# Depthwise convolution of a two-layer encoder: from a mix of PE and DVE taps to paired taps on PE alone

## The chip, the core and the metric
One core of one Trainium2 chip. The metric is device time in microseconds (us), from the first to the last instruction of one launch and what lies around it, as the median of several runs. PE is TensorE, PEld its weight loads, DVE VectorE, ACT ScalarE, POOL GpSimd; SP issues nearly all transfers.

## The reference
256 tokens of 1024 channels go through two layers. Each has a token-mixing part and a channel-mixing part (a dense SwiGLU in layer 0, the two best of eight experts in layer 1). The token mixing projects the normalised input to three groups that are computed apart and joined by one output projection: a pooling mixer (256 channels), a Conformer convolution (384 channels), and a spatial gate (384 channels). The convolution is what changes:

```python
def conformer_conv(p, conv_w, conv_b, ln_g, ln_b):     # p: (1, 256, 768), conv_w: (31, 384)
    val, gate = jnp.split(p, 2, axis=-1)
    glu = val * jax.nn.sigmoid(gate)
    y = depthwise_conv(glu, conv_w, width 31, padding 15) + conv_b
    return jax.nn.silu(layer_norm(y, ln_g, ln_b))
```

All is in float32.

## The kernel before, in words
The program is one straight list per engine. A scheduler orders each engine's instructions in advance by their place in the program and by when it thinks their inputs are ready; on the chip every engine runs its list in order and waits on semaphores. Buffers of one name are handed out in program order.

Weights come from memory in chunks of up to 1 MB into a ring of eleven buffers named `raw` (L109). A chunk for a precise product is split by ACT and DVE into a high and a low part (`wh`, L122, and `wl`, L123), and each product is three matmuls (`mm3`, L131 to L133). The modulation of the layers (`ada`) is a matrix-vector product that DVE accumulates chunk by chunk (L184; for the first quarters of layer 0 L256 and L259) and PE sums over partitions (L204, L265).

`mix_layer` (L327) is the token mixing, run once in each layer. In layer 0 its input projection is woven with the first modulation by the list `START` (`m` a quarter of the modulation, `h` a quarter of the hidden state, `A` and `B` chunks of the input projection); in layer 1 the chunks come one after the other, with modulation chunks between by `TICKS1`. With channels on partitions, 384 channels are three tiles `ct` of 128 x 256 tokens. The value half is copied to `glu` by ACT (L417), the sigmoid of the gate half goes to `mf` (L423), and POOL multiplies the two in place (L425), with 15 zero columns on each side.

Then come the spatial gate (L457 to L512), the convolution (L514 to L539), the pooling mixer (L541 to L570, on POOL but for one matmul, L566, and with `pd` in the two-buffer name `mf`), and the layer norm of the convolution: transposes (L576), statistics and normalisation on DVE with a small POOL part (L450 to L454), transposes back (L582), swish (L585) and `put`, which splits into high and low (L474, L475). The output projection takes its k-tiles in the order 6, 7, 0, 1, 4, 5, 2, 3; tiles 2 to 4 are the convolution's.

The convolution has two forms. The first `nchain` tiles (one in layer 0, two in layer 1) are a chain of 31 DVE operations each. For the others ACT scales the identity by one tap's weights, a diagonal of 128 x 128 per tap (L532), in two `raw` buffers per tile, and PE accumulates 31 matmuls over shifted views of `glu` (L536):

```python
dg.append(dt[:, j % 16 * P:(j % 16 + 1) * P])
nc.scalar.activation(out=dg[j], in_=ident, func=AF.Copy, scale=cl[:, w0 + j:w0 + j + 1])
...
nc.tensor.matmul(out=p[:, :S], lhsT=dg[j], rhs=glu[:, ct, j:j + S], start=j == 0, stop=j == TAPS - 1)
```

In the second layer's experts, half of the experts are narrow: two weight matrices are multiplied by the same 64 columns, into the two partition halves of one output (L1039).

Of the kernel before, what the change touches and what calls it, by code (L numbers as in the profile page):

```python
# [40 lines left out]
TICKS0, NCHAIN0 = (0, 0, 0, 0, 0, 0, 0, 0, 2, 2, 2, 2, 0), 1  # L41
TICKS1, NCHAIN1 = (0, 1, 0, 1, 1, 1, 1, 1, 1, 1), 2
# [5 lines left out]
NCOL = 48 + 8 + 8 + 2 + 3 * TAPS + 15  # L48
C_ADAB, C_MIXG, C_FFNG, C_PSC, C_CW = 0, 48, 56, 64, 66
C_CB = C_CW + 3 * TAPS  # L50
# [4 lines left out]
def trunk(ctx: ExitStack, tc: tile.TileContext, t, out):  # L55
# [28 lines left out]
    nc.vector.memset(mhalf, -0.5)  # L84

# [241 lines left out]
    def mix_layer(l, xn, ticks, nchain):  # L327
        cl = cols[l]
        with tc.tile_pool(name=f"mix{l}", bufs=1) as mp:
# [34 lines left out]
            glu = mp.tile([P, CT, S + TAPS - 1], F32, name="glu")  # L364
            nc.gpsimd.memset(glu, 0.0)
            if l:
# [5 lines left out]
                slab(t["in_last"][0], CW, 4, vals)  # L372
            else:
# [27 lines left out]
                for what in START:  # L401
                    q = int(what[1])
                    if what[0] == "m":
                        ada_first(q)
                    elif what[0] == "h":
                        hidden(xn, G, Sh, hh, hl, kps=(q,))
                        if q == 0:
                            heat(bank("dn"), 8)
                    elif what[0] == "A":
                        quarter(q, 0, ((0, vals, False), (CW, gates, False)))  # L410
                    else:
                        quarter(q, 1, ((CW, vs, True), (0, us, False)))
                spare["bank"] = "gu"
                later_ada()
            ds = vals
            for ct in range(CT):
                nc.scalar.copy(out=glu[:, ct, 15:15 + S], in_=ds[ct][0])  # L417
            ds = gates
            if l:
                slab(t["in_last"][1], CW, 4, ds)  # L420
            for ct in range(CT):
                sg = small.tile([P, S], F32, name="mf")
                nc.scalar.activation(out=sg, in_=ds[ct][0], func=AF.Sigmoid)  # L423
                gl = glu[:, ct, 15:15 + S]
                nc.gpsimd.tensor_tensor(out=gl, in0=gl, in1=sg, op=ALU.mult)  # L425
# [89 lines left out]
            for ct in range(nchain):  # L515
                w0 = C_CW + ct * TAPS
                nc.vector.tensor_scalar(out=cv[:, ct], in0=glu[:, ct, 0:S],
                                        scalar1=cl[:, w0:w0 + 1],
                                        scalar2=cl[:, C_CB + ct:C_CB + ct + 1],
                                        op0=ALU.mult, op1=ALU.add)  # L520
                for j in range(1, TAPS):
                    nc.vector.scalar_tensor_tensor(out=cv[:, ct], in0=glu[:, ct, j:j + S],
                                                   scalar=cl[:, w0 + j:w0 + j + 1], in1=cv[:, ct],
                                                   op0=ALU.mult, op1=ALU.add)
            for ct in range(nchain, CT):
                w0 = C_CW + ct * TAPS
                dg = []
                for j in range(TAPS):
                    if j % 16 == 0:
                        dt = raw.tile([P, CH], F32, name="raw")  # L530
                    dg.append(dt[:, j % 16 * P:(j % 16 + 1) * P])
                    nc.scalar.activation(out=dg[j], in_=ident, func=AF.Copy,  # L532
                                         scale=cl[:, w0 + j:w0 + j + 1])
                p = bank()
                for j in range(TAPS):
                    nc.tensor.matmul(out=p[:, :S], lhsT=dg[j], rhs=glu[:, ct, j:j + S],  # L536
                                     start=j == 0, stop=j == TAPS - 1)
# [4 lines left out]
            for ct in range(2):  # L542
# [16 lines left out]
                pd = small.tile([P, S], F32, name="mf")  # L559
# [49 lines left out]
    mix_layer(0, xn, TICKS0, NCHAIN0)  # L609
# [102 lines left out]
    mix_layer(1, xn, TICKS1, NCHAIN1)  # L712
# [531 lines left out]
```

## Time and profile before

| | |
|---|---|
| runs | 1353.39 us median of 3 (1353.2 to 1358.18) |
| the profiled execution | 1357.15 us, its span 1355.1 us |
| busy share of the span | PE 95%, PEld 69%, DVE 64%, ACT 47%, POOL 6% |
| granted TensorE clock | 0.977 in the mean |
| memory traffic | 466.15 MB, 344 GB/s in the mean |

Times in the rows count from the span's start. The first mixing layer ends near 138, the dense SwiGLU near 348, the second mixing layer near 457; the experts take the rest. Matmuls are pipelined, so the records of neighbours overlap: start to start tells the pace. One float32 matmul leaves two records. A granted clock of 1.00 is 2.4 GHz; a mean between 0.5 and 1 is a stretch with both levels.

### The profile page before, as it was taken

How to read it: one execution, taken by the hardware profiler on the slowest of the kernel's cores; microseconds unless marked ns; L12 is line 12 of the kernel's file. 1: busy time of each engine (PE TensorE's matmuls, PEld its weight loads, DVE VectorE, ACT ScalarE, POOL GpSimd, SP SyncE). 2: the span in 40 equal slices, each digit the busy share in tenths (PEclk: the TensorE clock that was granted, in tenths of full speed). 3: DMA queues.
4: the chain of work that ended last, by engine and by line, in shares of the span. 5: the costliest groups of instructions: out<-in, count | busy, mean ns of one | idle time of the engine just before them, and what ended most of it. 6: DMA issues, size and time to landing. Idle time of an engine off the chain costs nothing. (4 is left out here: it accounts for less than half of the span.)

```text
span 1355.1 us, 17989 instructions
## 1 busy us (share of the span) xinstructions
PE 1291.0 (95%) x6684; PEld 936.3 (69%) x6684; DVE 862.3 (64%) x1032; ACT 633.6 (47%) x919; POOL 77.1 (6%) x106
## 2 busy tenths in 40 slices
PE   6998899999897999999999999999999999999995
PEld 6986899998896888853368874447885336886431
DVE  6898886778698699850078873038885008876302
ACT  3563544434481587731257752237773125765101
POOL 1143100000125100000000000000000000000000
PEclk9998999999897999999999999999999999999997
DMA  9855895985573499989999998999998999999894
GB/s 372 318 223 209 341 401 191 401 306 193 206 280 126 176 345 374 354 325 422 421 421 421 393 348 358 421 421 421 421 401 345 410 420 421 421 419 363 367 420 163
DMA packets 71412, 466.15 MB, mean 344 GB/s; under 512 B 8596, under 2 KB 11284, under 8 KB 18968
## 3 DMA queue, kind: packets, MB, share of 16 engines
q1 hardware_dynamic: 71320, 464.95, 85.6%
q8 instruction: 54, 0.88, 0.3%
q14 instruction: 38, 0.31, 0.1%
HBM read 463.87 MB, written 1.05 MB: 343 GB/s over the span
## 5 line engine op out<-in xcount | busy, mean ns | idle before, releaser
L123 DVE TENSOR_TENSOR wl<-raw,wh 128x1024 fp32r<-128x1024 f32 (+1 forms) x454 | 528.1, 1206 | 99.3 <-ACT wh L122 92.8
L122 ACT CAST wh<-raw 128x1024 fp32r<-128x1024 f32 (+1 forms) x454 | 445.0, 1034 | 134.4 <-PE gu L132 45.0
L1039 PE MATMUL gu<-raw,big 128*64 128x512 f32 x896 | 204.9, 595 | 0.0
L1028 PE MATMUL gu<-wl,big 128*128 128x512 f32 x448 | 176.7, 394 | 3.0 <-DVE wl L123 2.5
L1026 PE MATMUL gu<-wh,big 128*128 128x512 f32 x448 | 175.2, 391 | 0.0
L1068 DVE TENSOR_TENSOR maf<-mx,mf 128x256 f32<-128x256 f32 x28 | 11.9, 425 | 231.0 <-PE dn L908 196.7
L1039 PEld LDWEIGHTS gu<-raw,big 128*64 128x64 f32 x896 | 63.1, 137 | 121.6 <-issue 119.8
L1023 PE MATMUL gu<-wh,big 128*128 128x512 f32 x448 | 142.5, 397 | 0.0
L131 PE MATMUL gu<-big,wh 128*128 128x256 f32 x464 | 133.0, 290 | 1.7 <-ACT big L299 1.3
L133 PE MATMUL gu<-big,wl 128*128 128x256 f32 x464 | 132.1, 286 | 0.6 <-DVE wl L123 0.6
L132 PE MATMUL gu<-big,wh 128*128 128x256 f32 x464 | 132.2, 286 | 0.0
L908 PE MATMUL dn<-raw,maf 128*64 128x512 f32 x448 | 110.2, 598 | 0.6 <-DVE maf L1068 0.6
L1042 ACT COPY mg<-gu 128x512 f32<-128x512 f32 x28 | 16.4, 585 | 196.8 <-PE gu L1039 196.8
L1028 PEld LDWEIGHTS gu<-wl,big 128*128 128x128 f32 x448 | 84.3, 188 | 26.1 <-DVE wl L123 7.8
L184 DVE SCALAR_TENSOR_TENSOR acc<-raw,cond,acc 128x1024 f32<-128x1024 f32 x74 | 97.3, 1315 | 1.0
L1023 PEld LDWEIGHTS gu<-wh,big 128*128 128x128 f32 x448 | 82.9, 189 | 19.8 <-ACT wh L122 3.2
L1026 PEld LDWEIGHTS gu<-wh,big 128*128 128x128 f32 x448 | 84.5, 189 | 16.9
L132 PE MATMUL dn<-wl,mah 128*128 128x512 f32 x224 | 91.1, 407 | 1.6 <-DVE wl L123 1.6
L131 PEld LDWEIGHTS gu<-big,wh 128*128 128x128 f32 x464 | 90.4, 196 | 3.1 <-ACT big L299 1.9
L133 PEld LDWEIGHTS gu<-big,wl 128*128 128x128 f32 x464 | 90.3, 195 | 0.8 <-DVE wl L123 0.8
L132 PEld LDWEIGHTS gu<-big,wh 128*128 128x128 f32 x464 | 90.4, 195 | 0.6 <-issue 0.2
L133 PE MATMUL dn<-wh,mal 128*128 128x512 f32 x224 | 88.9, 397 | 0.0
(235 smaller groups left out, 1577.7 us busy)
## 6 DMA issues: line engine op xcount, KB each, us to landing
raw<-in_experts SPq DMA_DIRECT2D x336, 1024.0 KB, 11.7
raw<-in_ada_pairs SPq DMA_DIRECT2D x24, 1024.0 KB, 7.6
raw<-in_ada_w SPq DMA_DIRECT2D x16, 1024.0 KB, 9.2
raw<-in_ffn_w_down SPq DMA_DIRECT2D x11, 1024.0 KB, 7.4
raw<-in_ffn_w_gate SPq DMA_DIRECT2D x10, 1024.0 KB, 11.1
raw<-in_ffn_w_up SPq DMA_DIRECT2D x10, 1024.0 KB, 9.0
raw<-in_w_out SPq DMA_DIRECT2D x8, 1024.0 KB, 6.9
raw<-in_in_first SPq DMA_DIRECT2D x8, 768.0 KB, 17.6
```

The source lines that it names most:

```text
L122: behind(lambda: nc.scalar.copy(out=h, in_=s), on_act)
L123: behind(lambda: nc.vector.tensor_tensor(out=l, in0=s, in1=f32(h), op=ALU.subtract), on_dve)
L131: nc.tensor.matmul(out=o, lhsT=lh, rhs=rh, start=first, stop=False, skip_group_check=True)
L132: nc.tensor.matmul(out=o, lhsT=lh, rhs=rl, start=False, stop=False, skip_group_check=True)
L133: return nc.tensor.matmul(out=o, lhsT=ll, rhs=rh, start=False, stop=last, skip_group_check=True)
L184: nc.vector.scalar_tensor_tensor(out=acc[0], in0=c[:, a], scalar=cond[:, k:k + 1], in1=acc[0], op0=ALU.mult, op1=ALU.add)
L908: nc.tensor.matmul(out=ds[0][q * HALF:(q + 1) * HALF], lhsT=a[:, 2 * i + h], rhs=w[:, h, q * 512:(q + 1) * 512], start=j == 0 and i == 0 a ...
L1023: nc.tensor.matmul(out=p, lhsT=eh[:, k], rhs=wh[a2], start=k == 0, stop=False, skip_group_check=True)
L1026: nc.tensor.matmul(out=p, lhsT=el[:, k], rhs=wh[a2], start=False, stop=False, skip_group_check=True)
L1028: nc.tensor.matmul(out=p, lhsT=eh[:, k], rhs=wl[a2], start=False, stop=k == KT - 1, skip_group_check=True)
L1039: nc.tensor.matmul(out=p[h * HALF:(h + 1) * HALF], lhsT=ef[:, k], rhs=w[:, a], start=k == 0, stop=k == KT - 1, skip_group_check=True)
L1042: nc.scalar.copy(out=g, in_=p)
```

## The change
All three tiles go to PE in both layers. `glu` gets a copy for each half of a tile's 128 channels; in each copy the 64 channels stand twice, on partitions 0 to 63 as they are and on 64 to 127 one token earlier, so that one matmul over 128 partitions applies two taps. A diagonal is then 128 x 64: two 64 x 64 diagonals above each other. 31 taps and a zero tap are 16 pairs, and the two channel halves are matmuls into the two partition halves of one output. The diagonals of one tile (32 x 64 columns) fill one `raw` buffer and are made by one POOL multiplication of a fixed pattern `twice` by the weights, both broadcast. The product of value and sigmoid is made by DVE from PSUM, four operations per tile, instead of ACT's copy and POOL's product. `pd` gets its own two buffers.

```diff
-TICKS0, NCHAIN0 = (0, 0, 0, 0, 0, 0, 0, 0, 2, 2, 2, 2, 0), 1
-TICKS1, NCHAIN1 = (0, 1, 0, 1, 1, 1, 1, 1, 1, 1), 2
+TICKS0 = (0, 0, 0, 0, 0, 0, 0, 0, 2, 2, 2, 2, 0)
+TICKS1 = (0, 1, 0, 1, 1, 1, 1, 1, 1, 1)
+PAIRT = (TAPS + 1) // 2
...
+    twice = const.tile([P, HALF], F32, name="twice")
+    nc.vector.tensor_tensor(out=twice, in0=ident[:, :HALF], in1=ident[:, HALF:], op=ALU.add)
...
-            glu = mp.tile([P, CT, S + TAPS - 1], F32, name="glu")
-            nc.gpsimd.memset(glu, 0.0)
+            glu = mp.tile([P, CT, 2, S + TAPS - 1], F32, name="glu")
+            for edge in (slice(0, 15), slice(14 + S, S + TAPS - 1)):
+                nc.gpsimd.memset(glu[:, :, :, edge], 0.0)
+            dgs = []
+
+            def diagonals():
+                for ct in range(CT):
+                    dg = raw.tile([P, CH], F32, name="raw").rearrange("p (m i) -> p m i", i=HALF)
+                    w0 = C_CW + ct * 2 * PAIRT
+                    nc.gpsimd.tensor_tensor(
+                        out=dg, in0=twice[:, None, :].to_broadcast([P, 2 * PAIRT, HALF]),
+                        in1=cl[:, w0:w0 + 2 * PAIRT].unsqueeze(2).to_broadcast([P, 2 * PAIRT, HALF]),
+                        op=ALU.mult)
+                    dgs.append(dg)
...
                 slab(t["in_last"][0], CW, 4, vals)
+                diagonals()
...
+                    if what == "h3":
+                        diagonals()
...
-            ds = vals
-            for ct in range(CT):
-                nc.scalar.copy(out=glu[:, ct, 15:15 + S], in_=ds[ct][0])
-            ds = gates
             if l:
-                slab(t["in_last"][1], CW, 4, ds)
+                slab(t["in_last"][1], CW, 4, gates)
             for ct in range(CT):
                 sg = small.tile([P, S], F32, name="mf")
-                nc.scalar.activation(out=sg, in_=ds[ct][0], func=AF.Sigmoid)
-                gl = glu[:, ct, 15:15 + S]
-                nc.gpsimd.tensor_tensor(out=gl, in0=gl, in1=sg, op=ALU.mult)
+                nc.scalar.activation(out=sg, in_=gates[ct][0], func=AF.Sigmoid)
+                for h in range(2):
+                    hs = slice(h * HALF, (h + 1) * HALF)
+                    for o in range(2):
+                        nc.vector.tensor_tensor(out=glu[o * HALF:(o + 1) * HALF, ct, h, 15 - o:15 - o + S],
+                                                in0=vals[ct][0][hs], in1=sg[hs], op=ALU.mult)
...
-            for ct in range(nchain):
...
-            for ct in range(nchain, CT):
...
+            for ct in range(CT):
                 p = bank()
-                for j in range(TAPS):
-                    nc.tensor.matmul(out=p[:, :S], lhsT=dg[j], rhs=glu[:, ct, j:j + S],
-                                     start=j == 0, stop=j == TAPS - 1)
+                for m in range(PAIRT):
+                    for h in range(2):
+                        nc.tensor.matmul(out=p[h * HALF:(h + 1) * HALF, :S], lhsT=dgs[ct][:, h * PAIRT + m],
+                                         rhs=glu[:, ct, h, 2 * m:2 * m + S], start=m == 0,
+                                         stop=m == PAIRT - 1, skip_group_check=True)
...
-                pd = small.tile([P, S], F32, name="mf")
+                pd = mp.tile([P, S], F32, name="pd", bufs=2)
```

The table of weights is laid out anew on the host to fit, with the zero tap.

## Rows read from the trace of the kernel before

**Rows 1.** The page: the span, and PE's busy time, its share of the span and its records.

```profile
span 1355.1 us, 17989 instructions
...
PE 1291.0 (95%) x6684; PEld 936.3 (69%) x6684; DVE 862.3 (64%) x1032; ACT 633.6 (47%) x919; POOL 77.1 (6%) x106
```

**Rows 2.** Busy time by stretch: the stretch, its length, then for each engine busy us and records, the granted clock, the DMA share and GB/s.

```profile
101.00:107.00 6.00, 2.54 (x13) 1.80 (x12) 5.96 (x5) 1.35 (x3) 5.08 (x4) 1.00 0.97 400
107.00:110.00 3.00, 3.00 (x12) 2.52 (x11) 2.93 (x3) 2.00 (x4) 1.65 (x2) 0.57 1.01 429
320.00:340.00 20.00, 20.00 (x126) 17.98 (x126) 18.03 (x17) 7.11 (x8) 0.00 (x0) 1.00 0.40 137
422.00:430.00 8.00, 2.75 (x7) 1.76 (x7) 8.00 (x11) 0.86 (x2) 3.33 (x5) 0.68 0.06 8
```

**Rows 3.** Groups of instructions by line and shape, from 0 to 110 us (layer 0): busy us and mean ns of one, then the idle time before them.

```profile
L532 ACT ACTIVATE raw<-ident,cols 128x128 f32<-128x128 f32 x62 | 18.8, 393 | 0.0
L522 DVE SCALAR_TENSOR_TENSOR cv<-glu,cols,cv 128x256 f32<-128x256 f32 x30 | 18.5, 617 | 0.9
...
L506 DVE SCALAR_TENSOR_TENSOR mf<-gu,cols,sgb 64x256 f32<-64x256 f32 x6 | 2.9, 482 | 0.8 <-POOL big L475 0.6
```

**Rows 4.** PE's timeline in layer 0: start, duration, the instructions, and in brackets the idle time before them and what ended it.

```profile
74.31 26.94 PE L536 MATMUL gu<-glu,raw 128*128 128x256 f32 x124
...
106.30 0.70 PE L566 MATMUL gu<-mf,pw 128*128 128x256 f32 x2 [3.46 <-POOL mf L564]
...
113.71 0.52 PE L582 MATMUL gu<-ident,tok 128*128 128x128 f32 x3 [2.40 <-DVE tok L454]
...
118.30 0.39 PE L131 MATMUL dn<-wh,big 128*128 128x512 f32 x1
...
123.53 0.40 PE L133 MATMUL mx<-wh,big 128*128 128x512 f32 x1
...
136.41 1.84 PE L204 MATMUL gu<-ones_c,acc 128*128 128x1 f32 x16
```

**Rows 5.** The same in layer 1; the last row is the last matmul of the output projection.

```profile
407.90 13.55 PE L536 MATMUL gu<-glu,raw 128*128 128x256 f32 x62
...
427.35 0.79 PE L132 MATMUL dn<-wl,big 128*128 128x512 f32 x1 [5.25 <-DVE wl L123]
...
432.81 1.33 PE L576 MATMUL gu<-ident,cv 128*128 128x128 f32 x5 [2.07 <-DVE cv L522]
...
457.18 0.40 PE L133 MATMUL mx<-wh,big 128*128 128x512 f32 x1
```

**Rows 6.** Who waited for whom from 0 to 130 us: us in total, times, the longest.

```profile
POOL acc L191 <- PE dn L265: 29.0, 1, 29.0
...
POOL mf L562 <- PE gu L566: 13.3, 1, 13.3
...
DVE mod L226 <- PE dn L265: 7.3, 4, 1.8
...
PE dn L265 <- DVE acc L259: 0.6, 2, 0.3
```

**Rows 7.** Weight loads of a narrow expert, two to a row.

```profile
660.00 0.14 PEld L1039 LDWEIGHTS gu<-raw,big 128*64 128x64 f32 x2 [0.29 <-issue]
660.43 0.14 PEld L1039 LDWEIGHTS gu<-raw,big 128*64 128x64 f32 x2 [0.29 <-issue]
```

**Rows 8.** POOL and DVE beside each other: POOL's product by its line (ns, min/median/max), then POOL's and DVE's timelines; first L184 and L123 while POOL was idle, then both at 379, then the taps without POOL (397.66) and with it (413.52).

```profile
L425 POOL TENSOR_TENSOR glu<-glu,mf x6: 639/1126/1712, 61.6 to 382.0; 128x256 f32<-128x256 f32 x6
...
55.89 1.82 DVE L123 TENSOR_TENSOR wl<-raw,wh 128x768 fp32r<-128x768 f32 x2
...
162.30 1.28 DVE L184 SCALAR_TENSOR_TENSOR acc<-raw,cond,acc 128x1024 f32<-128x1024 f32 x1
...
379.46 3.89 POOL L425 TENSOR_TENSOR glu<-glu,mf 128x256 f32<-128x256 f32 x3 [26.14 <-ACT mf L423]
...
378.57 2.86 DVE L184 SCALAR_TENSOR_TENSOR acc<-raw,cond,acc 128x1024 f32<-128x1024 f32 x2
381.36 2.80 DVE L123 TENSOR_TENSOR wl<-raw,wh 128x768 fp32r<-128x768 f32 x2
...
397.66 11.56 DVE L522 SCALAR_TENSOR_TENSOR cv<-glu,cols,cv 128x256 f32<-128x256 f32 x29
...
413.52 12.64 DVE L522 SCALAR_TENSOR_TENSOR cv<-glu,cols,cv 128x256 f32<-128x256 f32 x16
```

**Rows 9.** SP's timeline (its DMA issues) where chunks go to the ring, and the ACT cast that first needs one of the three chunks issued from 21.89 on.

```profile
21.89 5.00 SPq L109 DMA_DIRECT2D raw<-in_in_first  x3
...
31.25 0.33 SPq L109 DMA_DIRECT2D raw<-in_in_pool  x1
...
319.69 3.44 SPq L109 DMA_DIRECT2D raw<-in_in_last  x2
324.56 0.38 SPq L109 DMA_DIRECT2D raw<-in_ada_w  x1
...
43.40 0.83 ACT L122 CAST wh<-raw 128x768 fp32r<-128x768 f32 x1
```

**Rows 10.** The end of the dense SwiGLU: the last accumulation on DVE that PE's L204 sums, and that L204.

```profile
336.67 1.28 DVE L184 SCALAR_TENSOR_TENSOR acc<-raw,cond,acc 128x1024 f32<-128x1024 f32 x1
...
340.46 1.84 PE L204 MATMUL gu<-ones_c,acc 128*128 128x1 f32 x16
```

More of the change, by code (lines that the diff above doesn't have):

```diff
@@ L46 @@
 PRE, POST = 3, 1
-NCOL = 48 + 8 + 8 + 2 + 3 * TAPS + 15
+PAIRT = (TAPS + 1) // 2
+NCOL = 48 + 8 + 8 + 2 + 2 * CT * PAIRT + 15
 C_ADAB, C_MIXG, C_FFNG, C_PSC, C_CW = 0, 48, 56, 64, 66
-C_CB = C_CW + 3 * TAPS
+C_CB = C_CW + 2 * CT * PAIRT
 C_LG, C_LB, C_SG, C_SB = C_CB + 3, C_CB + 6, C_CB + 9, C_CB + 12
@@ L325, in quads, with mix_layer @@
         return bank(name).rearrange("p (a s) -> p a s", a=2)
-    def mix_layer(l, xn, ticks, nchain):
+    def mix_layer(l, xn, ticks):
         cl = cols[l]
@@ L514, in mix_layer @@
             cv = mp.tile([P, CT, S], F32, name="cv")
-            for ct in range(nchain):
[L516 to L524, printed above, removed]
-            for ct in range(nchain, CT):
-                w0 = C_CW + ct * TAPS
-                dg = []
-                for j in range(TAPS):
[L529 to L533, printed above, removed]
-                p = bank()
-                for j in range(TAPS):
-                    nc.tensor.matmul(out=p[:, :S], lhsT=dg[j], rhs=glu[:, ct, j:j + S],
-                                     start=j == 0, stop=j == TAPS - 1)
+            for ct in range(CT):
+                p = bank()
+                for m in range(PAIRT):
[3 more added lines that the diff above has]
+                                         stop=m == PAIRT - 1, skip_group_check=True)
                 nc.scalar.activation(out=cv[:, ct], in_=p[:, :S], func=AF.Identity,
@@ L607, in later_ada @@
         ada(0, "2", "3A")
-    mix_layer(0, xn, TICKS0, NCHAIN0)
+    mix_layer(0, xn, TICKS0)
     tick(len(queue), done=True)
@@ L711, in trunk @@
     nc.sync.dma_start(out=rb, in_=t["router_b"].broadcast_to([P, NE]))
-    mix_layer(1, xn, TICKS1, NCHAIN1)
+    mix_layer(1, xn, TICKS1)
     tick(len(queue), done=True)
@@ L1176, in col @@
         return _np.ascontiguousarray(v.reshape(v.shape[0], -1, P).transpose(0, 2, 1))
-    cw = a["conv_w"].transpose(0, 2, 1).reshape(DEPTH, CT, P, TAPS).transpose(0, 2, 1, 3)
+    taps = _np.zeros((DEPTH, 2 * PAIRT, CT * P), a["conv_w"].dtype)
+    taps[:, :TAPS] = a["conv_w"]
+    cw = taps.reshape(DEPTH, PAIRT, 2, CT, 2, HALF).transpose(0, 2, 5, 3, 4, 1)
     cols = _np.concatenate(
         [col(a["ada_b"]), col(a["mix_norm_g"]), col(a["ffn_norm_g"]), col(a["pool_scale"]),
-         cw.reshape(DEPTH, P, CT * TAPS), col(a["conv_b"]), col(a["conv_ln_g"]), col(a["conv_ln_b"]),
+         cw.reshape(DEPTH, P, 2 * CT * PAIRT), col(a["conv_b"]), col(a["conv_ln_g"]), col(a["conv_ln_b"]),
          col(a["sgu_ln_g"]), col(a["sgu_ln_b"])],
```

## The prediction
> **What bounds the kernel now.** I read the page first, then the busy time by stretch around the two convolutions, then PE's timeline there, then the waits, and last the DVE and POOL timelines wherever both were busy. The page says PE 1291.0 us of a span of 1355.1 [rows 1]. So PE is the engine to follow, and a gain has to shorten PE's work or one of its few gaps. Everything behind the second mixing layer (the experts) starts when that layer ends, and its loads pass through the same ring of places, so I carry each shift one to one to the end.
>
> Layer 0: from 74.31 PE runs 124 records of the convolution, 62 matmuls, in 26.94 us without a gap [rows 4], that is 0.434 us a matmul. ACT beside it builds 62 diagonals and DVE does 30 of the 31 taps of the third channel tile [rows 3]. Then PE waits 3.46 us for POOL, and later 2.40 us for the norm on DVE [rows 4]. The first wait starts further back: POOL's L562 waited 13.3 us for PE's L566 [rows 6], because `pd` of the second pooling tile needs the buffer that the first matmul, queued behind the convolution, still reads. After the gap the granted clock is 0.57 in the mean [rows 2], so part of the stretch runs at the lower of the two levels, 1.2 instead of 2.4 GHz.
>
> Layer 1: PE does one tile in 13.55 us, then waits 5.25 and 2.07 us [rows 5] for DVE, which is busy all of 422 to 430 while PE is busy 2.75 of 8 us [rows 2]: two DVE chains of taps set the end here.
>
> **PE's part.** The change needs 3 tiles x 16 tap pairs x 2 halves = 96 matmuls a layer. The narrow experts already run two column halves side by side: two 64-column loads start every 0.43 us with 512 columns streaming [rows 7]; one fp32 matmul is two such records, so a pair costs 0.86 there and 0.43 at 256 columns. Bounds for a pair: 0.43; 0.56 if its four loads of 0.14 came one behind the other and set the pace; 0.86 if the halves did not overlap. I take 0.44, nearest to the row of the same form: 48 x 0.44 = 21.1 us a layer.
> - Layer 0: 26.94 - 21.1 = 5.8 us gained.
> - Layer 1: 21.1 - 13.55 = 7.6 us more.
> The Trainium skill, "TensorE: Matmul & The Clock Gate", Part 3, says that a weight load overlaps a running matmul only when the row group differs; here both halves use all rows. The loads of rows 7 start inside running matmuls of the same rows, so the trace disagrees. What the rule would do is a rival below.
>
> **PE's gaps.** One output-projection matmul costs (123.53 - 118.30) / 23 = 0.227 us at full clock, so the 96 of a layer 21.8. In layer 0 the stretch from 101.25 (end of the convolution) to 136.41 is 35.2 us; with pooling, transposes and the gate's broadcast I count 25.3 of work at full clock, so 9.9 are waste: 3.46 + 2.40 idle and some 4.0 of half clock, split by me as 2.1 and 1.9 behind the two gaps.
> - `pd` gets its own two buffers, so the first gap goes: 3.46 + 2.1 = 5.6 us. The next in line is the norm chain, about 10 us behind the convolution; covered by 5 k-tiles x 12 matmuls x 0.227 = 13.6 us of projection that needs no convolution, if they stand in front of it in PE's order. In the trace they only partly do, hence the 2.40. I take half of that waste: 2.1 us. Bounds 0 and 4.3.
> - Layer 1: from 421.4 to the end of the last projection matmul are some 36.0 us for 24.0 of work (the same without the broadcast) [rows 5]; 12.0 are wasted, 7.3 of them idle, and DVE's chains are the cause. I leave a norm gap of 2.1 and gain 9.9. Less the 7.6 above: 2.3 us.
> Gains so far: 5.8 + 5.6 + 2.1 + 2.3 = 15.8 us.
>
> **What the change takes back: POOL.** Three multiplications of 128x2048 a layer. The nearest row is 128x256 in 0.64 us at best [rows 8], so 8 x 0.64 = 5.1 each and 15.4 us a layer alone. (The Trainium skill, "GPSIMD Engine Reference", section 3.1, gives 4497 ns for a two-input operation of that length: 13.5 a layer, and the sum below would be about 1 us better. No run here shows that shape.)
> But POOL does not run alone. From 379.46 three POOL operations took 3.89 us, double their best, and DVE beside them needed 2.86 and 2.80 us for what costs 2.56 and 1.82 elsewhere [rows 8]: DVE lost 1.28 us, a third of the overlap. Small DVE operations lose more: 16 taps in 12.64 us against 29 in 11.56 [rows 8], about half. At the first price, with POOL overlapping contending DVE work for some 18 us, DVE loses 6 us a layer.
> When? The operations take three places of the raw ring, in program order, as soon as these come free.
> - Layer 0: that is where the loads at 21.89 (three in_first chunks) were issued [rows 9], so POOL works from about 22 to 46. There DVE sums the modulation, PE multiplies it out at once (PE waited only 0.6 for DVE, DVE 7.3 us for PE's four answers [rows 6]) and the next hidden state needs it: a loop without slack, so I charge all 6.
> - Layer 1: places come free at 319.69 to 324.56 [rows 9], so POOL works from 320 to 344, beside DVE at 18.03 of 20 us [rows 2]. The last accumulation, at 336.67, ends 2.6 us before PE's L204 at 340.46 [rows 10] uses it: 6 - 2.6 = 3.4 us.
> Bounds a layer: 0 (POOL gives way, or runs in DVE's gaps) to half of 30.7 us, 15.3.
>
> **The rest.** The displaced loads go to the next free places: the three in_first chunks from 21.89 to about 30 to 36 (before, the ring's next issue is at 31.25); ACT first casts one at 43.40 [rows 9], so I cost it at nothing; without that cover it is a few us. Behind the new POOL work stands the memset of L191, which before sat 29.0 us waiting for PE [rows 6]; SP's transfer into the same tile waits for it, and behind that on SP stand the next modulation chunks and the spatial gate's tables. None of them is used before the convolution's neighbours, so I cost this at nothing; without that cover it is up to some 5 us. Later the ring is better off: three held places instead of four in layer 0. ACT loses 62 and 31 diagonals, on no path now. DVE gets 12 half-tile products of 0.48 [rows 3], 5.8 us a layer, ahead of weight splits in its order, and loses the taps; I charge 1 us in all, bounds 0 and 5. The memset, copies and `twice` are nothing.
>
> **Sum.** 15.8 - 6 - 3.4 - 1 = 5.4 us. The profiled execution took 1357.15 (span 1355.1), 3.8 above the median of the runs, 1353.39; I subtract from the median: 1348.0.
>
> **Rivals.**
> - *POOL gives way* (DVE loses little): for it, that POOL doubled its time at 379.46. 1353.4 - 14.8 = 1338.6. Chance 0.25.
> - *The norm takes the place of the gaps*: PE's order is fixed in advance, and in both layers the second transposes come too early, at their present 2.40 plus half clock. The half that I credited falls away in layer 0 (2.1) and as much again in layer 1 (2.2): gains 5.8 + 5.6 + 0.1, less 10.4: 1352.3. Chance 0.13.
> - *Contention wins*, the slower side: the loss at the price of the taps, half of 30.7 us a layer, 15.3 + 12.7 = 28 against 14.8: up to 1366.6. It decides from a total loss above 14.8 us; for it rows 8's taps, against it that DVE's operations from 22 to 46 are long ones. Chance 0.18.
> - *The halves do not run side by side* as said: 41.3 us a layer, 1348 + 40.4 = 1388. Against it rows 7. Chance 0.03. With the loads unhidden as well, 48 x (0.43 + 0.56) a layer, 1401: chance 0.01. That is the skill's rule on row groups, named above.
> My forecast has the remaining 0.40; its own range is 1343 to 1353.
>
> **How the numbers follow.** About 0.5% (6.8 us, so 1346.6 and 1360.2) is what a measurement of this kernel can tell from no change. Faster: 0.24 of the first rival and 0.18 of the forecast: 0.42. Slower: 0.16 of the contention rival and the 0.04: 0.20. Same: the rest, 0.38. The range reaches from just under the first rival, 1336, to 1360, in the middle of the contention rival.
>
> **What would show it.** Right: conv matmuls 128x64 in 20 to 22 us a layer; no wait of L562 for L566; POOL tensor products of 5 to 10 us at 22 and 320; modulation loop longer than before between 22 and 50; PE's wait at L204 in front of layer 1. Wrong: PE's pace in the conv above 0.5 us a pair; POOL's products at another time, or as quick as 5.1 beside busy DVE; no later end of the input projection.

## The result, and the profile after

The changed kernel took 1365.97 us in the median of its runs (1365.19 to 1368.49), the kernel before 1355.79 beside it (1353.2 to 1358.28): a ratio of 1.0077, with a 95% interval of 1.0056 to 1.0098. That is slower by 10 us, and outside the range of the forecast. The profiled execution took 1366.27, its span is 1364.5. First the page's span and first part, where [rows 1] stand for the kernel before.

```profile
span 1364.5 us, 18241 instructions
...
PE 1292.0 (95%) x6882; PEld 928.3 (68%) x6882; DVE 837.2 (61%) x964; ACT 606.3 (44%) x823; POOL 94.5 (7%) x108
```

PE is busy for as long as before, on more and narrower records. DVE has 25 us less work, ACT 27 less, POOL 17 more. Nothing in these sums is a loss, so the time went into waits. Busy time by stretch (columns as in [rows 2]):

```profile
20.00:40.00 20.00, 13.45 (x76) 13.24 (x76) 15.77 (x17) 4.33 (x7) 11.69 (x3) 0.67 0.84 344
...
320.00:340.00 20.00, 17.74 (x124) 16.29 (x122) 19.58 (x9) 7.92 (x9) 12.84 (x3) 1.00 0.22 77
```

From 20 to 40 us PE is busy 13.45 of 20, at a granted clock of 0.67: it idles, and then works partly at the lower of its two levels. Before, it was busy 19.47 there. Line numbers shift by 4 up to `mix_layer` (L265 is now L269, L256/L259 are L260/L263, L123 is L127, L184 is L188, L204 is L208), by 19 in the norm's helper and the spatial gate (L450 is L469, L501 is L520), and by 2 or 3 from the convolution on (L536 is L538, L582 is L585). POOL's products are L377; here they are on POOL's timeline:

```profile
21.52 4.01 POOL L377 TENSOR_TENSOR raw<-twice,cols 128x2048 f32<-128x2048 f32 x1 [10.44 <-DVE wl L127]
27.61 4.06 POOL L377 TENSOR_TENSOR raw<-twice,cols 128x2048 f32<-128x2048 f32 x1 [2.09 <-DVE acc L263]
33.63 3.62 POOL L377 TENSOR_TENSOR raw<-twice,cols 128x2048 f32<-128x2048 f32 x1 [1.95 <-DVE acc L263]
...
324.79 4.67 POOL L377 TENSOR_TENSOR raw<-twice,cols 128x2048 f32<-128x2048 f32 x1 [81.51 <-DVE acc L188]
330.62 4.54 POOL L377 TENSOR_TENSOR raw<-twice,cols 128x2048 f32<-128x2048 f32 x1 [1.16 <-DVE wl L127]
336.33 3.62 POOL L377 TENSOR_TENSOR raw<-twice,cols 128x2048 f32<-128x2048 f32 x1 [1.16 <-DVE acc L188]
```

and beside them DVE (the row at 42.03 is the same pair of operations as at 21.96, with POOL idle):

```profile
21.96 4.25 DVE L260 TENSOR_SCALAR acc<-raw,cond 128x512 f32<-128x512 f32 x2
26.13 7.42 DVE L263 SCALAR_TENSOR_TENSOR acc<-raw,cond,acc 128x512 f32<-128x512 f32 x6
37.30 0.23 DVE L230 TENSOR_TENSOR mod<-dn,cols 128x2 f32<-128x2 f32 x2 [3.75 <-PE dn L269]
...
42.03 0.88 DVE L260 TENSOR_SCALAR acc<-raw,cond 128x512 f32<-128x512 f32 x2
...
325.89 5.79 DVE L127 TENSOR_TENSOR wl<-raw,wh 128x1024 fp32r<-128x1024 f32 x2
331.60 9.43 DVE L188 SCALAR_TENSOR_TENSOR acc<-raw,cond,acc 128x1024 f32<-128x1024 f32 x2
```

The pair of L260 takes 4.25 us beside a product and 0.88 without. Six of L263 take 7.42 instead of 4.06. At the FFN's end two splits (L127) take 5.79 instead of 2.4 and two additions (L188) 9.43 instead of 2.56 [rows 8]. POOL's products take 4.0 to 4.7 us where a DVE operation is well under way as they begin, and 3.62 where none is or where it has only just begun (at 336.33, 0.04 us behind the second of L188, which then is the one that waits). So POOL is hardly slowed, and DVE stands almost still. Then PE, beside the products in layer 0 and at the end of its mixing layer:

```profile
32.94 0.58 PE L269 MATMUL dn<-ones_c,acc 128*128 128x1 f32 x2 [6.55 <-DVE acc L263]
...
34.27 2.99 PE L269 MATMUL dn<-ones_c,acc 128*128 128x1 f32 x14
...
85.91 1.08 PE L538 MATMUL gu<-glu,raw 128*64 128x256 f32 x6
...
89.52 20.51 PE L538 MATMUL gu<-glu,raw 128*64 128x256 f32 x186
109.96 1.13 PE L569 MATMUL gu<-pd,pw 128*128 128x256 f32 x4
...
121.77 0.87 PE L585 MATMUL gu<-ident,tok 128*128 128x128 f32 x3 [6.13 <-DVE mv L471]
122.29 0.78 PE L137 MATMUL mx<-wh,big 128*128 128x512 f32 x1
```

The convolution takes 1.08 + 20.51 = 21.6 us, POOL's matmul (now L569) follows it at once, and then PE waits 6.13 us for the normalization, where it waited 3.46 and 2.40 before [rows 4].

**Where the time went.** Four marks can be read from every kernel's timelines. A: DVE's fourth L230 (the end of layer 0's modulation loops). C: the first down-projection matmul of the dense SwiGLU (its operand is `fah`). D: PE's L208 at the SwiGLU's end. E: the first L312 of the residual behind layer 1's mixing. (In the kernels without the new convolution these lines are L226, L204 and L308.) The table has the length of each stretch in the profiled execution, and the median of the timed runs with its ratio to the kernel before on the same chip.

| kernel | A | A to C | C to D | D to E | span | median us, ratio (95%) |
|---|---|---|---|---|---|---|
| before | 51.2 | 147.1 | 142.2 | 113.1 | 1355.1 | |
| changed | 61.5 | 144.5 | 148.0 | 108.6 | 1364.5 | 1366.0, 1.0077 (1.0056 to 1.0098) |
| E1 diagonals on ACT, late | 52.4 | 150.2 | 141.6 | 108.6 | 1354.6 | 1358.8, 1.0017 (0.9998 to 1.0035) |
| E2 on DVE, same place | 53.7 | 147.5 | 141.7 | 109.6 | 1354.0 | 1356.0, 0.9999 (0.9982 to 1.0016) |
| E3 before + POOL products | 60.7 | 147.3 | 149.2 | 110.0 | 1370.2 | 1372.7, 1.0122 (1.0095 to 1.0148) |
| E4 before + `pd` | 52.3 | 149.9 | 142.2 | 114.3 | 1361.5 | 1363.1, 1.0039 (1.0018 to 1.0060) |
| E5 changed + order | 60.6 | 145.9 | 150.0 | 108.1 | 1366.7 | 1368.7, 1.0090 (1.0072 to 1.0109) |
| E6 DVE late + order | 52.4 | 146.7 | 141.7 | 108.4 | 1349.6 | 1354.4, 0.9975 (0.9962 to 0.9989) |
| E7 before + `pd` + order | 53.2 | 147.1 | 142.1 | 114.4 | 1359.5 | 1358.9, 1.0023 (1.0006 to 1.0039) |
| E8 E6, chunks ahead | 50.8 | 153.3 | 141.7 | 108.5 | 1354.2 | 1359.4, 1.0035 (1.0018 to 1.0052) |
| E9 E6, chunks behind products | 51.1 | 146.3 | 141.6 | 108.6 | 1351.2 | 1351.9, 0.9977 (0.9966 to 0.9988) |
| E10 E9, more of both | 52.0 | 160.2 | 141.7 | 108.7 | 1364.4 | 1367.2, 1.0087 (1.0070 to 1.0105) |
| E13 DVE late, old order | 51.2 | 149.5 | 141.7 | 108.5 | 1351.0 | 1356.6, 1.0007 (0.9995 to 1.0018) |
| E14 POOL late | 62.6 | 146.4 | 141.7 | 119.3 | 1372.1 | 1374.1, 1.0136 (1.0111 to 1.0160) |
| E15 E9, ACT and DVE | 51.1 | 152.9 | 141.7 | 109.7 | 1357.2 | 1360.0, 1.0031 (1.0018 to 1.0044) |
| E16 E9, two more chunks | 52.4 | 145.5 | 141.7 | 109.9 | 1351.1 | 1352.7, 0.9976 (0.9964 to 0.9987) |
| E17 changed, products cut | 61.8 | 144.0 | 141.6 | 109.7 | 1358.5 | 1358.9, 1.0020 (1.0008 to 1.0032) |

From before to changed: +10.3 in A, -2.6 from A to C (layer 0's convolution and all behind it), +5.8 from C to D, -4.5 from D to E (layer 1); +9.0 at E, and 9.4 in the span. One kernel varies too: A was 60.2 in E12 and 61.8 in E17, which are the same, and from E to the end the rows lie between 899.9 and 903.6. A profiled execution isn't always a median one: E13's is the fastest of its twelve. The medians of the kernel before differ by up to 2.6 us from one set of experiments to another, so runs of different sets are compared by their ratios.

### The profile page after: what moved, and what is told of

The parts are those of the page before. It is cut to its first block, busy times and chain, and to the rows that moved or that the text cites. A ratio compares the mean times of both kernels' runs of the same rounds, so it can differ in the third digit from the quotient of the medians.

```text
span 1364.5 us, 18241 instructions
## 1 busy us (share of the span) xinstructions
PE 1292.0 (95%) x6882; PEld 928.3 (68%) x6882; DVE 837.2 (61%) x964; ACT 606.3 (44%) x823; POOL 94.5 (7%) x108
## 5 line engine op out<-in xcount | busy, mean ns | idle before, releaser
L127 DVE TENSOR_TENSOR wl<-raw,wh 128x1024 fp32r<-128x1024 f32 (+1 forms) x454 | 529.7, 1209 | 111.4 <-ACT wh L126 104.4
L136 PE MATMUL gu<-big,wh 128*128 128x256 f32 x464 | 131.2, 284 | 1.7 <-DVE big L304 1.7
L135 PE MATMUL gu<-big,wh 128*128 128x256 f32 x464 | 130.7, 286 | 1.3 <-ACT big L303 1.3
L188 DVE SCALAR_TENSOR_TENSOR acc<-raw,cond,acc 128x1024 f32<-128x1024 f32 x74 | 103.7, 1401 | 1.0
```

Of the source, the lines that this page charges most:

```text
L127: behind(lambda: nc.vector.tensor_tensor(out=l, in0=s, in1=f32(h), op=ALU.subtract), on_dve)
L135: nc.tensor.matmul(out=o, lhsT=lh, rhs=rh, start=first, stop=False, skip_group_check=True)
L136: nc.tensor.matmul(out=o, lhsT=lh, rhs=rl, start=False, stop=False, skip_group_check=True)
L188: nc.vector.scalar_tensor_tensor(out=acc[0], in0=c[:, a], scalar=cond[:, k:k + 1], in1=acc[0], op0=ALU.mult, op1=ALU.add)
```

## The experiments

**Theory T1:** POOL's products shut DVE out and so cost A and C to D. **R:** the ring places that they hold delay the loads. **N:** the normalization's wait takes the place of the gap that goes. **D:** DVE's work, or the loads, hold layer 0's end wherever the wait shows.

### Who pays for POOL's products: E1, E2, E3

E3 adds the products to the kernel before and nothing else; E2 moves them to DVE; E1 to ACT, just ahead of the convolution.

```diff
 E2   -  nc.gpsimd.tensor_tensor(out=dg, ...)
      +  nc.vector.tensor_tensor(out=dg, ...)
 E1   +  for m in range(2 * PAIRT):   # called ahead of the convolution
      +      nc.scalar.activation(out=dg[:, m], in_=twice, func=AF.Copy,
      +                           scale=cl[:, w0 + m:w0 + m + 1])
 E3   +  nc.gpsimd.tensor_tensor(out=raw_tile, in0=twice (broadcast),
      +                          in1=cols (broadcast), op=ALU.mult)  # in before, x3 a layer
```

> The kernel before, its taps and convolution untouched, with three POOL products of the changed kernel's form (128x2048, both operands broadcast) added at the two places of the text where the changed kernel has them; their tiles are used by nothing, so a ring place is held only until the product is done. T1: slower by what the changed kernel lost before its convolutions, +10 to +16 us, 1366 to 1372. R (places held until the convolution): under +3 us. N: no change.

> The changed kernel with the same three broadcast products a layer at the same place of the text, on VectorE instead of POOL. T1: VectorE pays about 3 x 2.4 us (a 1024-wide two-input operation takes 1.2 us) in a layer instead of 0.85 x 11.7 = 10 us, so the loss shrinks but does not go: -2 to -6 us, 1360 to 1364. R (ring places): the places are taken at the same point, no change, 1364 to 1368. That it is the planner's order on PE: no forecast of a sign.

> The changed kernel with the diagonals built by ScalarE (96 scaled copies of 128x64 a layer, issued in the text just ahead of the convolution, as the kernel before did with its 62 and 31 copies of 128x128), POOL's products gone; the same ring places, taken later. Theory T1 (POOL's broadcast products shut VectorE out: +10.3 us by the second and fourth loops of mix layer 0, +5.7 us at layer 1's entry): both losses go, so the fourth L230 starts near 51 us instead of 61.5 and the time falls by 10 to 16 us, to 1350 to 1356, less what 96 copies at 0.3 us (29 us of ACT a layer, 19 us before) put in front of ACT's casts. Rival R (the three ring places and the later loads): places are taken later, so this too would gain in layer 0's loops, but L1's entry stays. Rival N (the pair's wait is the normalization, and the convolution's place on PE): nothing changes before 85 us, the time stays at 1364 to 1368.

E3 is 17 us slower than before, with before's convolution: what T1 says, a little above its 10 to 16. Its POOL timeline:

```profile
20.78 4.01 POOL L1248 TENSOR_TENSOR raw<-twice,cols 128x2048 f32<-128x2048 f32 x1 [9.79 <-DVE wl L123]
26.87 4.06 POOL L1248 TENSOR_TENSOR raw<-twice,cols 128x2048 f32<-128x2048 f32 x1 [2.08 <-DVE acc L259]
```

and its DVE timeline, two rows with a product beside them and the same two without:

```profile
21.22 4.25 DVE L256 TENSOR_SCALAR acc<-raw,cond 128x512 f32<-128x512 f32 x2
25.39 7.41 DVE L259 SCALAR_TENSOR_TENSOR acc<-raw,cond,acc 128x512 f32<-128x512 f32 x6
...
41.29 0.88 DVE L256 TENSOR_SCALAR acc<-raw,cond 128x512 f32<-128x512 f32 x2
42.08 4.07 DVE L259 SCALAR_TENSOR_TENSOR acc<-raw,cond,acc 128x512 f32<-128x512 f32 x6
```

4.25 and 7.41 us against 0.88 and 4.07: the changed kernel's numbers to 0.01 us. A is at 60.7, C to D at 149.2. The places are free as soon as a product is done there, so R can't explain it. E2 and E1 have A at 53.7 and 52.4 and C to D at 141.7 and 141.6, near the 51.2 and 142.2 of before: most of the first loss goes, and all of the second. (E2 did better than T1 said, 1356.0 for 1360 to 1364; E1 worse, 1358.8 for 1350 to 1356 and what the copies cost ACT.) Yet neither beats the kernel before. A to C is 147.5 and 150.2 us against 147.1, although PE's convolution has 5.3 us less to do (in E1 it waits 1.9 us for ACT's copies). So a second thing failed.

### Broadcast, length, place: E11, E12, E17, E14

E11 repeats E3 with plain operands (`x` times `x`), E12 and E17 cut each product of the changed kernel into 8, E14 calls the uncut products ahead of the convolution in the text.

```diff
 E12  -  nc.gpsimd.tensor_tensor(out=dg, ...)                     # 128x2048
      +  for m in range(0, 2 * PAIRT, 4):
      +      nc.gpsimd.tensor_tensor(out=dg[:, m:m + 4], ...)     # 128x256
```

> The kernel before with three POOL products of 128x2048 at the places of the dummy products, their operands not broadcast (x times x, both 128x2048). If the broadcast operands are what shuts VectorE out: POOL takes more than 4.1 us for each, VectorE's two operations beside one take under 3 us (4.25 with broadcast) and the loss is under 8 us. If any two-input product of that width does: the same 15 to 17 us as the dummy products, 1368 to 1374.

> The changed kernel with each product cut into 8 of 128x256 (24 a layer), the same operands otherwise. If VectorE is shut out for the length of one instruction and gets its turn between two: POOL's total grows, VectorE's stretches at 21.96 and 26.13 us (4.25 and 7.42 us) shrink to under 3 and 6 us, 1358 to 1363. If it loses in proportion to POOL's busy time whatever the length: no change, 1364 to 1369.

POOL's timeline in E11:

```profile
21.21 3.98 POOL L1248 TENSOR_TENSOR raw<-x 128x2048 f32<-128x2048 f32 x1 [9.94 <-DVE wl L123]
27.27 4.04 POOL L1248 TENSOR_TENSOR raw<-x 128x2048 f32<-128x2048 f32 x1 [2.08 <-DVE acc L259]
```

DVE's in E11:

```profile
21.64 4.22 DVE L256 TENSOR_SCALAR acc<-raw,cond 128x512 f32<-128x512 f32 x2
25.79 7.39 DVE L259 SCALAR_TENSOR_TENSOR acc<-raw,cond,acc 128x512 f32<-128x512 f32 x6
```

POOL's in E12, all 24 pieces in one row:

```profile
21.72 22.84 POOL L378 TENSOR_TENSOR raw<-twice,cols 128x256 f32<-128x256 f32 x24 [10.89 <-DVE wl L127]
```

DVE's in E12:

```profile
22.16 1.60 DVE L260 TENSOR_SCALAR acc<-raw,cond 128x512 f32<-128x512 f32 x2
23.67 6.21 DVE L263 SCALAR_TENSOR_TENSOR acc<-raw,cond,acc 128x512 f32<-128x512 f32 x6
```

Broadcasting is not the cause: E11 has 4.22 and 7.39 us, and A at 60.7. (It took 1375.1 us, 1.1 beyond what was expected; in layer 1 `x` is ready later, so its products ran there, from 360.21 on, and D to E is 120.8.) Cut, the 24 products take 22.84 us, 0.95 each, and DVE's pair 1.60, its six 6.21 (under 6 was expected): the two engines take turns, one instruction each. Layer 0 gains nothing by that (A at 60.2): summed over its operations DVE loses 6.6 us there, as with the uncut products (6.7), in a loop where PE waits for DVE. At the FFN's end DVE loses 5.9 us instead of 10.3, spread over 28 us, and C to D is back at 141.7: that much is hidden there. E12 took 1358.0 in one execution, and E17 timed it:

> The changed kernel with each product cut into 8 of 128x256, timed. By the one execution seen: 1356 to 1360, that is 6 to 10 us under the changed kernel with nothing else altered; if that execution was a lucky one: 1362 to 1367.

1358.9 us, 7 under the changed kernel, as expected. Cutting pays back what the FFN's end had lost.

> The changed kernel with POOL's products just ahead of the convolution in the text in both layers, where VectorE without taps is busy 4 to 13 of 20 us. If the loss is VectorE shut out where it is the bound (first loops, the FFN's end): the fourth L230 is back at 51 to 52 us and the mark at the FFN's end at 342 to 345, the time 1354 to 1360. If POOL's 4 us beside it cost the same anywhere: 1362 to 1368.

E14 missed both of its forecasts, since its products did not run late. Ahead of them in POOL's queue stood only a memset (L195), which waited for PE until 40.05, and then the ring places:

```profile
40.96 3.64 POOL L377 TENSOR_TENSOR raw<-twice,cols 128x2048 f32<-128x2048 f32 x1
45.56 3.63 POOL L377 TENSOR_TENSOR raw<-twice,cols 128x2048 f32<-128x2048 f32 x1 [0.96 <-DMA acc<-in_ada_b]
50.95 4.01 POOL L377 TENSOR_TENSOR raw<-twice,cols 128x2048 f32<-128x2048 f32 x1 [1.76 <-DVE wl L127]
...
373.46 10.59 POOL L377 TENSOR_TENSOR raw<-twice,cols 128x2048 f32<-128x2048 f32 x2 [10.51 <-DMA pw<-in_pool_w]
384.94 4.68 POOL L377 TENSOR_TENSOR raw<-twice,cols 128x2048 f32<-128x2048 f32 x1 [0.89 <-DVE wl L127]
```

They ran inside layer 0's loops all the same (A at 62.6), and in layer 1 at its start, where D to E became 119.3. One of them took 6.0 us (from 373.46, the first of the pair in its row): three DVE splits went first. That POOL costs less beside an idle DVE wasn't tried.

### What took layer 0's gain: E4 to E7

E4 gives the kernel before `pd`'s own buffers and nothing else. E5 changes only DVE's order behind layer 0's convolution in the changed kernel; E7 has both in the kernel before; E6 has that order, and the products on DVE ahead of the convolution.

```diff
 E4   -  pd = small.tile([P, S], F32, name="mf")
      +  pd = mp.tile([P, S], F32, name="pd", bufs=2)
 E5   +  made = token_norm(cn[:, n], ...)        # its last DVE instruction
      +  if l == 0:                              # issued behind it:
      +      more["after"] = [(None, None)] * 2 + [(None, made)] * 6   # w_out splits
      +      more["late"] = [made] * 12                                # ada additions
```

> The kernel before with one part of the change alone: the pooling result pd has two buffers of its own instead of sharing two with mf. The step of the prediction (the gap of 3.46 us and the low clock behind it go): -3 to -6 us in layer 0, up to -5 more in layer 1, 1345 to 1352. N (the wait for the normalization takes the gap's place, the stretch from the convolution's end to the output projection's end stays at 35 us): within 1.5 us of before, 1354 to 1357.

PE's timeline in E4, behind the convolution:

```profile
103.71 1.03 PE L566 MATMUL gu<-pd,pw 128*128 128x256 f32 x4
...
116.99 0.87 PE L582 MATMUL gu<-ident,tok 128*128 128x128 f32 x3 [8.37 <-DVE tok L454]
```

POOL's matmul follows the convolution without a gap, and PE then waits 8.37 us for the normalization. The step that I priced at 5.6 us gained is 5 us slower alone (1.0039; +5.1 at E), which neither forecast allowed for. Of the 5.1, 1.1 stand in A, ahead of the step, 2.8 between A and C and 1.2 in layer 1. In E4 the convolution ends at 103.88 and DVE comes to the statistics (L450) at 114.06, behind two splits and four additions that begin at 105.96. The changed kernel, whose convolution ends at 110.03, shows the same on DVE's timeline:

```profile
107.38 2.74 DVE L127 TENSOR_TENSOR wl<-raw,wh 128x1024 fp32r<-128x1024 f32 x2 [2.37 <-ACT wh L126]
110.05 0.74 DVE L185 TENSOR_SCALAR acc<-raw,cond 128x1024 f32<-128x1024 f32 x1
110.82 4.71 DVE L188 SCALAR_TENSOR_TENSOR acc<-raw,cond,acc 128x1024 f32<-128x1024 f32 x3
115.46 1.21 DVE L127 TENSOR_TENSOR wl<-raw,wh 128x1024 fp32r<-128x1024 f32 x1
116.59 1.27 DVE L188 SCALAR_TENSOR_TENSOR acc<-raw,cond,acc 128x1024 f32<-128x1024 f32 x1
117.90 1.03 DVE L469 BATCH_NORM_STATS2 st<-gu 128x6 f32<-128x384 f32 x2
```

The statistics (117.90) stand in DVE's fixed order behind three splits and five additions that begin at 107.38, and these behind 2.37 us of waiting for ACT's cast.

> The changed kernel with VectorE's order after layer 0's convolution changed alone: of w_out's eight half splits two stay ahead of the convolution's normalization and six are issued behind it, as are the 12 ada additions of the output projection's ticks. Theory N (what layer 0 gained up to the convolution's end is waited out at the normalization: 6.13 us, then half clock, because L469's statistics stand behind splits and additions in VectorE's order): the wait at L585 falls under 3 us and its half clock goes, convolution's end to output projection's end from 35.0 to 27 to 30 us, the time falls by 5 to 8 us to 1358 to 1361; POOL's loss stays. Rival D (VectorE's total work behind the convolution bounds the stretch, so the same splits come late elsewhere): the wait moves to the output projection, within 2 us of the changed kernel, 1364 to 1368.

> The kernel before, taps and convolution untouched, with pd's own buffers and the order of the two runs above. N: the price of layer 0's gap and of the normalization's wait without the new convolution: 6 to 9 us under the run with pd alone, 1353 to 1357, and 0 to 5 under the kernel before; what the run with the products on VectorE and this order has beyond it is what the convolution itself brings (5.8 us in layer 0 and 2.3 in layer 1 by the prediction). D: as pd alone, 1360 to 1364.

> The changed kernel with both causes taken away: the three products a layer on VectorE just ahead of the convolution in the text (2.3 us each, where it idles) and the order of the run before. T1 and N: POOL's 10 to 16 us and 5 to 8 us of the normalization's wait go, 1344 to 1349, faster than the kernel before by 0.5 to 0.9%. If D holds: 1352 to 1357, as with the products on VectorE alone.

In E5 the wait is 1.45 us and the FFN starts 5.3 us earlier (144.47 against 149.80), as N says; but the first down-projection comes at 206.5 against 206.0, and the run is no faster (1.0090 against 1.0077). Two of PE's waits in it:

```profile
114.42 0.52 PE L588 MATMUL gu<-ident,tok 128*128 128x128 f32 x3 [1.45 <-DVE tok L473]
...
156.55 0.58 PE L137 MATMUL gu<-big,wl 128*128 128x256 f32 x1 [3.62 <-DVE wl L127]
```

The wait moved to the FFN's entry, to the splits that now stand late. This is D. Three pairs of runs show it when A to C is split at L208, the end of the output projection. From the convolution's end to L208 the order takes off 5.5 us (35.0 to 29.5, changed to E5), 7.2 (36.4 to 29.2, E4 to E7) and 6.1 (35.6 to 29.5, E13 to E6); from L208 to C it puts on 6.9, 5.8 and 3.3. E7 gained 2 us on E4 by the ratios, within their intervals, where N said 6 to 9. E6 has both causes away and is faster than before, by 3 us where 7 to 12 were forecast; its 1354.4 is what D said.

### Filling DVE's idle time: E8, E9, E10, E13, E15, E16

Without taps DVE idles during the convolution (2.74 of 10 us busy at 90 to 100 in E6). These runs put ada additions there.

```diff
 E8   TICKS0 = (..., 4, 2, 2, 0, 0) for (..., 2, 2, 2, 2, 0): chunks ahead of the products
 E9   +  diagonals()                 # on DVE, ahead of the convolution
      +  if l == 0: tick(2)          # two chunks behind them; TICKS0 = (..., 2, 2, 2, 0, 0)
 E10  tick(4), and 4 splits of w_out ahead of the normalization instead of 2
 E13  E6 without the order
 E15  E9, products 2 and 3 by 64 ACT copies a layer as in E1
 E16  E9, and tick(2) once more behind the convolution's text
```

> As the run with products on VectorE and the new order, and with two more of the eight ada chunks' additions put ahead of layer 0's convolution (ticks 4, 2, 2, 0 in place of 2, 2, 2, 2), where VectorE without taps is idle. If the additions behind the normalization still delay the output projection: 1 to 4 us less than that run; if not: the same, or up to 2 us more where the last product comes late for the convolution.

> As the run with the products on VectorE and the new order (1354.4 us), with two of the six ada chunks behind layer 0's convolution put ahead of it, after the three products, so that VectorE's idle time during the convolution (it was busy 2.74 of 10 us at 90 to 100) takes 4 additions of 1.25 us. Theory E (the FFN's entry is what binds layer 0: VectorE, busy 10 of 10 us from 110 to 130, is behind with additions and splits, and the first use of the FFN's activations cannot come before about 199 us, whatever the convolution gains): the first down-projection of the FFN moves from 199.1 to 194 to 196 us, the time to 1349 to 1352. Rival L (the loads: the 16 queues move 400 GB/s from 140 to 200 us and the ring of 11 places was full before): stays at 198 to 200, 1353 to 1356.

> As the run before, with four of the chunks and two more of w_out's half splits ahead of the normalization (10 additions and 4 splits during the convolution). E: another 2 to 4 us, 1346 to 1350, if the loads come in time; where they don't, the statistics wait behind them and it loses up to 4 us, 1353 to 1357. L: 1353 to 1357.

> The products on VectorE just ahead of the convolution in the text, VectorE's order left to the planner (no ops put behind the normalization). Against the run with the products on VectorE at their old place (1356.0 us): if the three ring places held from the first loops on are what makes the later loads, and so the statistics, late, 3 to 6 us less, 1350 to 1353; against the run with the order (1354.4): if it is the order, 2 to 6 us more, 1356 to 1360.

> The fastest order so far (1351.9 us), with the second and third product of each layer built by ScalarE in 64 copies (19 us a layer, where it was busy 0.4 to 2.3 of 10 us from 70 to 100) and the first on VectorE: 4.6 us of VectorE's 70 to 85 us less. If VectorE's load around the convolution still binds: 1347 to 1351. If ScalarE's copies come late for the convolution: up to 3 us more, 1352 to 1355.

> The fastest order so far (1351.9 us), with two more ada chunks (4 additions, 5 us) taken from behind layer 0's convolution into its time, and the gate's matrix products behind the convolution on TensorE (in the run that lost, they stood ahead of it and TensorE waited 17 us for VectorE). If VectorE's work between convolution and FFN entry holds the gain: the first down-projection comes at 192 to 195 us instead of 197.4 and the time is 1347 to 1350. If the loads hold it: 197 to 200, 1351 to 1355; if the additions come late for the statistics, up to 3 us more than that.

E8 lost 5 to 8 us to E6, where 2 was the most expected: with the additions ahead, the second product came to stand behind the spatial gate's last operations on DVE, for which DVE idled 4.75 us until POOL's `put`, and PE waited 7.26 us in the convolution. E9, with the products first, has the lowest median, 1351.9 us, and 0.9977 of the kernel before (0.9966 to 0.9988): it beats both kernels, as E6 does at 0.9975. E10 lost 15 us to it (4 was the most expected): the gate's matmul of the finished accumulation was put ahead of the convolution on PE:

```profile
100.52 3.73 PE L241 MATMUL gu<-acc,ones 128*128 128x512 f32 x4 [17.09 <-DVE acc L188]
```

E15 lost 7 (3 was the most expected), since ACT's copies came late: PE waited 2.77 and 2.63 us for them. E13 stays at E2's time (1.0007 against 0.9999), so early or late ring places make no difference with the products on DVE: R falls, within some 2 us. Its wait for the normalization is 7.83 us, and the order is worth 4 us (E6, 0.9975). The filling is worth nothing that the ratios show (E9, E16). E9's first down-projection comes at 197.4, between the two forecasts, and its 1351.9 us is in E's range; but against E6 its ratio is unchanged, and E16, with more of the same, has 197.9 and 1352.7, as the loads' side said. What is left shows at the FFN's entry in E9 (columns as in [rows 2]):

```profile
136.00:146.00 10.00, 5.22 (x30) 4.13 (x31) 9.54 (x12) 4.99 (x7) 1.55 (x2) 0.90 1.02 414
146.00:156.00 10.00, 10.00 (x55) 10.00 (x55) 5.00 (x9) 1.00 (x2) 0.00 (x0) 0.58 1.02 416
```

and in E16's stretches, same columns:

```profile
120.00:130.00 10.00, 9.35 (x41) 7.37 (x40) 8.60 (x9) 2.27 (x3) 0.80 (x1) 1.00 0.01 2
...
140.00:150.00 10.00, 6.27 (x32) 5.33 (x33) 10.00 (x12) 4.93 (x7) 0.00 (x0) 0.79 1.02 423
150.00:160.00 10.00, 10.00 (x77) 10.00 (x76) 6.11 (x10) 3.01 (x4) 0.00 (x0) 0.87 1.02 416
```

After PE's idle 4.8 us the granted clock is 0.58 for ten. DVE is busy there in both, and the DMA queues stand still from 120 to 130 and run full from 140 on. Which of the two binds was not separated.

## Why the prediction was wrong

- **PE's part was right.** I took 0.44 us a pair, 21.1 us a layer; measured 21.6 and, in layer 1, 20.9. The two column halves run side by side. Layer 0's 26.94 fell by 5.3 us (I said 5.8).
- **Layer 1 was right.** I said 2.3 us and left a norm gap of 2.1; PE's wait there was 1.40. From the convolution's first matmul to E the changed kernel takes 43.0 us, 45.6 before: 2.6 gained. It is 43.0 to 43.1 in every run with the new convolution and 45.2 to 47.0 in those with the old one. The rest of the 4.5 us from D to E stands ahead of the convolution (65.6 us from D, 67.4 before). E3, with the old convolution, has 64.8 there, so what makes it stays open.
- **When POOL would work was right:** from 21.52 and 324.79 us, for 22 and 320. That they took 4.0 to 4.7 us beside a busy DVE was one of my signs of being wrong (5.1 or less).
- **The first step that failed is POOL's price.** From the row at 379.46 [rows 8] I read that POOL doubles and DVE loses a third of the overlap: 6 us in layer 0, 3.4 at layer 1's entry. It is the other way round: a product keeps its own 3.62 us plus the rest of the DVE operation in flight, and DVE does nothing for all of it. In layer 0 two products took 3.4 us each from DVE. The third fell on a DVE that waited 3.75 us for PE; PE, having waited 6.55 us, ran at a low clock (0.67 from 20 to 40), and its 14 matmuls from 34.27 took 2.99 us. A came 10.3 us later in all; that the 3.6 beyond DVE's loss are PE's low clock is argued, not shown. At the FFN's end 3.4 and 6.9 us were lost, and 5.8 came through. Together 16.1, beyond the 14.8 from which my contention rival decides. It was right that DVE loses more than a third, but not in its price, half of POOL's 30.7 us a layer, 28 us of loss in all; that the time, 1366.0, is so near to its 1366.6 is luck: a smaller loss (16.1) met smaller gains (7.1 for 14.8). The row had small instructions, where turns alternate; read as "DVE loses POOL's own time", it would have given up to 15.4 us a layer at my 5.1 a product, and up to 10.9 at the 3.62 measured.
- The Trainium skill, "SBUF — State Buffer", section "Who interferes with whom", says that a DVE operation with two SBUF inputs and a GpSimd operation that reads SBUF exclude each other for a whole instruction, the loser fully blocked. The trace agrees for L263, L127 and L188, which have two (5.79 us for 2.4 of work); L260, with one and a column of scalars, was shut out too (4.25 for 0.88), as the section says can happen to tensor_scalar in a two-port mode; no run shows which mode it was in. I had not weighed the rule.
- **The second step that failed is the gap.** I credited `pd` with 5.6 us and the norm with half its waste, because the norm chain, next in line, would be "covered by 5 k-tiles x 12 matmuls x 0.227 = 13.6 us of projection that needs no convolution, if they stand in front of it in PE's order". They don't: in PE's order 17 of these matmuls, 4.1 us, stand in front of the transposes. (Tile 5, counted in the 13.6, even comes behind the convolution's tile 4 in the program.) Then PE waits for what DVE has ahead of the statistics. From the convolution's end to L208 it took 35.0 us, before 35.2: 0.1 gained where I said 7.7. My norm rival had the mechanism, at a price of 2.1 us in layer 0.
- **Layer 0's shorter convolution arrived only in part.** Its end came 48.5 us behind A, before 50.1: 1.5 of the 5.3 us. PE waited 0.22 and 1.04 us for the spatial gate's normalization around the convolution's start, where before it did not wait, and the clock from A on was 0.93, before 1.00. I had charged 1 us for the glu products on DVE (12 in 5.2 us, for 5.8). The cause stays open: E12 and E17, the same kernel, differ by 1.5 us in that stretch. With 1.0 us behind L208, layer 0 gave 2.6 us of the 12.5 forecast.
- Also wrong: that the gain of a gap is carried one to one. A to C stays between 144 and 150 us whether the gap is at POOL's matmul, the normalization or the FFN's entry (E4, E5, E6). DVE's order took 2.8 us off it in E7 (against E4) and E6 (against E13), and put 1.4 on in E5 (against the changed kernel). One reading was off by little: the slack ahead of L204 [rows 10] is 2.5 us, not 2.6.
- The sum: -5.4 forecast, +9.0 measured at E. Of the 14.4 between, layer 0's gain is 9.9, POOL 6.7, and layer 1 gives 2.2 back.

## What to carry to other kernels

Where DVE has work, price a POOL elementwise operation at its own time taken from DVE, and place it by what stands ahead of it in its queue and by its buffers, not by its place in the text; if DVE has slack there, cut it into pieces. Before crediting a wait that goes, read what stands ahead of the next waiter, in its own engine's fixed order and in that of the engine that serves it. A split like the table's, by marks that every variant has, tells apart losses that a sum hides.

## What the runs showed of the hardware

A POOL product of 128x2048 takes 3.62 us alone, 4.0 to 4.1 beside DVE operations of 512 columns and 4.5 to 4.7 beside those of 1024 (once 6.0, in E14): it waits for the one in flight, then holds DVE off to its end. Pieces of 128x256 take turns with DVE, at 0.95 us each in the mean of 24. The same product takes DVE 2.29 us, and 32 scaled copies of 128x64 take ACT 7.9 (a third of this row of E1; after the count its busy us and mean ns):

```profile
L378 ACT ACTIVATE raw<-twice,cols 128x64 f32<-128x64 f32 x96 | 23.8, 336 | 0.0
```

Broadcast operands change none of this (E11). The Trainium skill, "GPSIMD Engine Reference", section 3.1, gives 4497 ns for the product on GpSimd and 2293 on DVE: the second agrees, the first is above the 3.62 us measured here, which decides.
